# The last 1024 hidden columns of a squared-ReLU MLP by seven products instead of eight

## The chip, the cores and the metric

The kernel runs on one core of a Trainium2 chip. The metric is the device time of one execution in microseconds. A core has TensorE for matmuls, VectorE (DVE), ScalarE (ACT) and GpSimd (POOL) for the rest, and queues from which DMAs are issued: that of SyncE (SP), of GpSimd and of ScalarE. TensorE reads its operands from SBUF and writes to PSUM, which ScalarE and VectorE read.

## The reference, cut to what matters

The reference is one layer of a decoder block on 512 tokens of width 1024: a token mixer (gated linear attention and latent attention in parallel, merged by gates), a layer norm, the MLP, a layer norm. The change lies in the MLP, with `w_ff1` of 1024 x 4096 and `w_ff2` of 4096 x 1024:

```python
h = layer_norm(DEEPNORM_ALPHA * h + mix, ln1_g[l], ln1_b[l])
ff = jnp.square(jax.nn.relu(h @ w_ff1[l])) @ w_ff2[l]
h = layer_norm(DEEPNORM_ALPHA * h + ff, ln2_g[l], ln2_b[l])
```

## The kernel before

Everything is float32. Each operand of a large product is split into a high part `hi` (fp32r, written by ScalarE's copy, L185 in `pump`, L111 in `split`) and a low part `lo` (the rest, by a subtraction on VectorE, L186 or L112). A product is three matmuls: hi x hi, hi x lo, lo x hi, accumulated in PSUM.

**The stream of weights.** All weights are listed ahead in `stream`, in the order in which they are used, as items of 512 KB (128 partitions x 1024 columns). `pump(i)`, called ahead of item `i`, issues the DMAs of items up to `i + DMA_AHEAD` on SP's queue (L173) into one of three `wraw` tiles, and the splits of items up to one further into one of two `whi` and two `wlo` tiles. Items marked `res`, and those whose `home` is `"a"`, go to tiles of the shared pool `"A"` (24 tiles of 4 KB per partition). An item with a `src` has no DMA: its tile is loaded elsewhere. Pool `"B"` has 22 tiles of 2 KB; the split activations `h1T` occupy 16 of them from the layer norm to the end of the first MLP product. PSUM has eight banks, four tagged `mm` and four `px`.

**The order.** Small generators (`spawn`, `tick`) are advanced between matmuls, so that their instructions are listed among them. The list order is a priority. The framework's scheduler then fixes the order of instructions on each engine with its own estimates of time, and an instruction may be issued well ahead of its place in the list if its operands and a buffer are free.

**The MLP.** It goes in four chunks of 1024 hidden columns (`for ci in range(FC)`). In each, the first product (`gemm_fm`, L238 to L240) makes the hidden values with columns on partitions: eight blocks of k, eight blocks of 128 columns, three matmuls of 512 tokens. `ev_h` applies relu (L1296) and a square. In the first three chunks the second product runs by seven products instead of eight (`win_f2`, L1268 to L1270): 14 steps of 12 matmuls, whose weight tiles `wq` are loaded by `win_load` on GpSimd's queue (L1213) and summed by `win_sums`. Its results are copied from PSUM to `ev` tiles (L1280) and added to the rows `res` by accumulating DMAs, again on GpSimd's queue (L1282). In the last chunk `ev_h` squares on ScalarE (L1310) and on GpSimd (L1311) and subtracts on VectorE (L1312), and the second product is plain (`gemm_tm`, L271 to L273, by pairs of token blocks, then the third and the fourth block), ending in the layer norm `ln2`.

**The gate product.** One other product already runs by seven products: the second half of the gates (`gemm_unit` with the key `"g1"`, L1016 to L1018). Its operands `h` and `w` are cut into 2 x 2 quarters. `op_sums` forms the four sums of the quarters of `h` and splits them (L965 to L972); `u_load` loads weight quarters and adds a second one by an accumulating DMA (L988, L990); `u_sum` makes the other weight sums on VectorE (L324). The products follow `FMO`: 11, 21, t1, 22, t2, t3, t4, each of 48 matmuls of 256 tokens. Between them the banks are combined by copies on ScalarE and subtractions on VectorE (L1023 to L1036).

Of the kernel before, what the change touches and what calls it, by code (L numbers as in the profile page):

```python
# [19 lines left out]
P = 128  # L20
T = 512
# [31 lines left out]
def tile_hybrid_block(ctx: ExitStack, tc: tile.TileContext, I, out, dbg=None):  # L53
# [108 lines left out]
    def pump(i):  # L162
        while st["dma"] < min(len(stream), i + 1 + DMA_AHEAD):
            e = stream[st["dma"]]
            st["dma"] += 1
            if "src" in e:
                continue
            raw = A([P, e["nk"], T * 2 // e["nk"]], F32, "wraw")
            for sl, src, cw in e["dmas"]:
                dst = raw[:, sl, :e["n"]]  # L170
                if cw is not None:
                    dst = dst.rearrange("p (h c) -> p h c", c=cw)
                nc.sync.dma_start(dst, src)  # L173
            e["raw"] = raw
        while st["spl"] < min(len(stream), i + 2 + SPLIT_AHEAD):
            e = stream[st["spl"]]
            if st["spl"] > i + e.get("ahead", SPLIT_AHEAD) and not e["res"]:
                break
            nk, n = e["nk"], e["n"]
            hi, lo = [A([P, nk, T * 2 // nk], F32R, w) for w in HOME["a" if e["res"] else e.get("home", "w")]]  # L180
            raw = e["src"]() if "src" in e else e.pop("raw")
            with ExitStack() as gates:
                for g in st["gates"]:
                    gates.enter_context(tc.issue_after(g.ins))
                st["ins"] = act(hi[:, :nk, :n], raw[:, :nk, :n], AF.Copy)  # L185
                vtt(lo[:, :nk, :n], raw[:, :nk, :n], f(hi[:, :nk, :n]), op=ALU.subtract)  # L186
# [121 lines left out]
    UNITS = {"g1": ("w_in", C_G + D)}  # L308
# [8 lines left out]
    def u_src(key, i, j, hf):  # L317
# [4 lines left out]
    def u_sum(key, a, to, hf, x):  # L322
        t = WQ[key, (to, hf)] = WQ[key, (a, hf)]
        vtt(t, t, x, op=ALU.add)  # L324


    for key in UNITS:
        PL[key] = []
        for op, _ in FMO:
            for hf in range(2):  # L330
                PL[key].append(len(stream))
                e = {"nk": 2, "n": T, "res": False}
                if op[0] != "t":
                    e["dmas"] = [(slice(0, 2), u_src(key, int(op[0]) - 1, int(op[1]) - 1, hf), None)]
                else:
                    e["src"] = lambda q=(key, (op, hf)): WQ[q]
                if op == "22":
                    e["post"] = lambda raw, q=(key, "t1", "t2", hf): u_sum(*q, raw)
                elif op == "t2":
                    e["post"] = lambda raw, q=(key, "t2", "t4", hf): u_sum(*q, WQ[key, ("21", q[3])])  # L340
                stream.append(e)
    plan_qr(0)
# [27 lines left out]
    F1 = [((0, 4), (4, 2), (6, 2))] + [tuple((b, 2) for b in range(0, 8, 2))] * 2 + [((0, 4), (4, 4))]  # L370
# [3 lines left out]
    for ci in range(FC):  # L374
# [610 lines left out]
    def u_load(key, op):  # L985
        for hf in range(2):
# [5 lines left out]
    def gemm_unit(key, ops, evac, after=None):  # L992

        bank, e1, e5, u2 = {}, {}, {}, {}
        nk = 2
        for n, (op, ph) in enumerate(FMO):
            items = PL[key][2 * n:2 * n + 2]
            for g in range(2):
                bk = ("a" if ph in (0, 3, 6, 4) else "b", g)
                opens = ph in (0, 2, 1)  # L1000
                if opens:
                    bank[bk] = (PX if ph == 1 else MM)()
                o = bank[bk]
                for hf, it in enumerate(items):
                    pump(it)
                    hi, lo = stream[it]["w"]
                    for pp in range(nk):
                        while len(ops) <= nk * hf + pp:
                            tick(3)
                        xh, xl = ops[nk * hf + pp][ph]  # L1010
                        for a in range(2):
                            c = slice((2 * g + a) * P, (2 * g + a + 1) * P)
                            oa = o[:, a * 256:(a + 1) * 256]
                            first = opens and hf == 0 and pp == 0 and a == 0
                            last = hf == 4 // nk - 1 and pp == nk - 1
                            mm(oa, hi[:, pp, c], xh, start=first, stop=False, skip_group_check=True)  # L1016
                            mm(oa, hi[:, pp, c], xl, start=False, stop=False, skip_group_check=True)  # L1017
                            mm(oa, lo[:, pp, c], xh, start=False, stop=last, skip_group_check=True)  # L1018
                        if pp % 2:
                            tick(3)  # L1020
# [3 lines left out]
                elif ph == 1:  # L1024
                    vtt(e1[g], o, e1[g], op=ALU.add)
                    evac(0, 0, g, e1[g], None)
# [3 lines left out]
                elif ph == 3:  # L1030
# [3 lines left out]
                    evac(1, 0, g, u2[g], None)  # L1034
                elif ph == 6:
                    vtt(e5[g], e5[g], o, op=ALU.subtract)  # L1036
                    evac(1, 1, g, e5[g], None)
                elif ph == 4:
                    evac(0, 1, g, o, None)
            if after:  # L1040
                after(op)

# [209 lines left out]
    def win_f2(ci, hid):  # L1252
        bank = {}
        for n, (op, hf, ph) in enumerate(WIN):
# [28 lines left out]
            if n == 9 and ci + 1 < FC - 1:  # L1283
                win_load(ci + 1)

    WT = {}
    for ci in range(FC):
# [6 lines left out]
        def ev_h(a, ps):  # L1294
            r = B([P, T], F32, "relu")
            act(r, ps, AF.Relu)  # L1296
            if win:
                if a % 2 == 0:
                    hid.append({"R": A([P, 2, T], F32, "hr")})
                ops = hid[-1]  # L1300
                R = ops["R"]
                act(R[:, a % 2, :], r, AF.Square)
                if a % 2:
                    h1 = A([P, 2, 2, 256], F32R, "h1p")
                    split(R[:, :, :256], h1[:, 0], h1[:, 1])
                    ops[0], ops[1] = [(h1[:, 0, i], h1[:, 1, i]) for i in range(2)]
                    spawn(win_hid(R, ops))
                return
# [4 lines left out]
            hid.append(hh)  # L1313
# [15 lines left out]
        else:  # L1329
            bg, bb = bcast_row("ln2_g"), bcast_row("ln2_b")  # L1330
            gemm_tm(PL["f2last"], hid, T, ev_res, tts=(0, 1))
# [67 lines left out]
```

## Time and profile before

| what | value |
|---|---|
| median of three runs | 901.83 us (900.83 to 902.12) |
| profiled execution, its own time | 901.97 us |
| its span | 900.2 us |
| granted TensorE clock | 0.998 |
| instructions on TensorE | 4652 matmuls |
| busy share of VectorE, ScalarE, GpSimd | 65%, 47%, 20% |
| second product of the third chunk | 766.9 to 805.0 us of the span |
| first product of the last chunk | 805.0 to 848.5 us |
| plain second product of the last chunk | from 848.5 us |

The span runs from the first to the last instruction of the profiled execution; the execution's time is 1.8 us longer. Times within the profile are counted from the span's start. In the view of groups, a row gives the line, the engine, the operation and the tiles (out<-in), the count, busy time and mean duration. In the view of waits a row says which engine and line waited for which, in total, how often, and the longest. A row of the timeline gives the start, the duration, the engine and the instruction, and in brackets the idle time before it with what ended it. A row of the table by stretches gives the stretch and its length, then the busy time and count of TensorE, its weight loads, VectorE, ScalarE and GpSimd, then the granted clock, the DMA share and the rate in GB/s.

### The profile page before, as it was taken

Reading aid. Unit: us, or ns where it says so; the run is one execution under the profiler, and the core shown is the slowest. Engines: PE = TensorE matmul, PEld = TensorE weight load, DVE = VectorE, ACT = ScalarE, POOL = GpSimd, SP = SyncE. Lnnn points to the kernel's source line nnn. Section 1 sums busy time; section 2 is a strip of 40 time slices with the busy share of each in tenths; the row PEclk is TensorE's granted clock in tenths of the full one; section 3 lists DMA queues with packets and bytes.
Section 4 is the critical chain, followed back from the end, with each engine's and each line's share of the span. In section 5 each row is a group of like instructions: output and inputs, shape, how many; then the busy total and the mean of one; then the engine's idle time right before and its main releaser. Section 6 shows DMA issues by size and latency. Waiting matters only on the chain.

```text
span 900.2 us, 12161 instructions
## 1 busy us (share of the span) xinstructions
PE 880.9 (98%) x4652; PEld 755.8 (84%) x4652; DVE 585.5 (65%) x953; ACT 427.3 (47%) x729; POOL 178.0 (20%) x196
## 2 busy tenths in 40 slices
PE   5999999999999999999999999999999999999996
PEld 5988888888889988888888888988888888888885
DVE  7835855577876645747756797997557646723565
ACT  5556443443546543445644423466367546733410
POOL 0103442444531010100000002104400520142200
PEclk9999999999999999999999999999999999999999
DMA  7414323216225623121207518005941990594311
GB/s 241 124 47 159 129 65 94 71 47 155 81 71 195 175 88 105 43 60 53 94 24 277 191 49 302 1 1 151 296 115 32 261 243 24 117 209 108 128 68 73
DMA packets 64776, 107.25 MB, mean 119 GB/s; under 512 B 7840, under 2 KB 27680, under 8 KB 64720
## 3 DMA queue, kind: packets, MB, share of 16 engines
q1 hardware_dynamic: 51344, 75.57, 26.3%
q0 software_dynamic: 11456, 27.27, 13.0%
q10 hardware_dynamic: 1920, 3.66, 1.2%
q8 instruction: 36, 0.59, 0.3%
q14 instruction: 20, 0.16, 0.1%
HBM read 89.18 MB, written 4.72 MB: 104 GB/s over the span
## 4 chain that ended last, share of the span: by engine, by line
PE 96%; DVE 2%; DMA 1%; ACT 1%; issue 0%; SPq 0%; DVEq 0%
PE mm L238 14%; PE mm L240 14%; PE mm L239 14%; PE mm L271 7%; PE mm L273 7%; PE mm L272 7%; PE px L1269 2%; PE px L1270 2%; PE px L1268 2%; PE px L723 2%; PE mm L1269 2%; PE mm L1270 2%; PE mm L1268 2%; PE mm L1018 1%; PE mm L1016 1%; PE mm L1017 1%
## 5 line engine op out<-in xcount | busy, mean ns | idle before, releaser
L186 DVE TENSOR_TENSOR wlo<-wraw,whi 128x1024 fp32r<-128x1024 f32 (+1 forms) x102 | 115.3, 1131 | 131.6 <-ACT whi L185 124.0
L185 ACT ACTIVATE whi<-wraw 128x1024 fp32r<-128x1024 f32 (+1 forms) x102 | 98.2, 962 | 109.5 <-PE mm L239 63.3
L238 PE MATMUL mm<-h,whi 128*128 128x512 f32 x352 | 137.6, 392 | 0.0
L239 PE MATMUL mm<-h,whi 128*128 128x512 f32 x352 | 137.3, 390 | 0.0
L240 PE MATMUL mm<-h,wlo 128*128 128x512 f32 x352 | 130.5, 390 | 0.0
L1282 POOL DMA_DIRECT2D res<-ev x48 | 42.1, 1018 | 187.5 <-ACT ev L1280 151.6
L238 PEld LDWEIGHTS mm<-h,whi 128*128 128x128 f32 x352 | 66.0, 188 | 13.5
L240 PEld LDWEIGHTS mm<-h,wlo 128*128 128x128 f32 x352 | 66.0, 188 | 13.5
L239 PEld LDWEIGHTS mm<-h,whi 128*128 128x128 f32 x352 | 66.1, 188 | 13.3
L272 PE MATMUL mm<-wlo,h 128*128 128x512 f32 x128 | 50.3, 393 | 0.0
L273 PE MATMUL mm<-whi,h 128*128 128x512 f32 x128 | 50.1, 392 | 0.0
L271 PE MATMUL mm<-whi,h 128*128 128x512 f32 x128 | 49.7, 403 | 0.0
L185 ACT ACTIVATE xh<-wraw 128x1024 fp32r<-128x1024 f32 (+1 forms) x28 | 27.1, 985 | 36.8 <-PE mm L273 16.5
L662 POOL TENSOR_TENSOR rp<-rp 128x256 f32<-128x256 f32 x32 | 31.6, 987 | 61.2 <-ACT E L667 44.8
L1296 ACT ACTIVATE relu<-mm 128x512 f32<-128x512 f32 x32 | 18.8, 595 | 49.3 <-PE mm L240 49.2
L186 DVE TENSOR_TENSOR wlo<-wq,whi 128x1024 fp32r<-128x1024 f32 x20 | 24.5, 1225 | 24.2 <-ACT whi L185 24.2
L391 POOL TENSOR_TENSOR mv<-mv,mhalf 128x1 f32<-128x1 f32 x4 | 4.6, 1154 | 172.4 <-DVE mv L390 172.4
L186 DVE TENSOR_TENSOR xl<-wraw,xh 128x1024 fp32r<-128x1024 f32 (+1 forms) x28 | 31.2, 1128 | 8.9 <-ACT xh L185 8.7
L669 DVE TENSOR_TENSOR M<-E,qk 128x512 f32<-128x512 f32 x32 | 27.8, 868 | 14.1 <-ACT E L667 14.1
L667 ACT ACTIVATE E<-rp 128x512 f32<-128x512 f32 x32 | 20.4, 638 | 24.9 <-POOL rp L663 24.9
L663 POOL TENSOR_TENSOR rp<-rp 128x256 f32<-128x256 f32 x32 | 28.2, 883 | 8.9 <-ACT q L692 6.7
L273 PEld LDWEIGHTS mm<-whi,h 128*128 128x128 f32 x128 | 24.0, 188 | 5.0
(405 smaller groups left out, 2415.3 us busy)
## 6 DMA issues: line engine op xcount, KB each, us to landing
wraw<-in_w_ff_dram SPq DMA_DIRECT2D x40, 512.0 KB, 4.5
wraw<-in_w_in_dram SPq DMA_DIRECT2D x38, 512.0 KB, 3.5
wq<-in_w_ff_dram POOLq DMA_DIRECT2D x24, 512.0 KB, 9.4
res<-ev POOLq DMA_DIRECT2D x48, 256.0 KB, 6.6
wraw<-in_w_o_gla_dram SPq DMA_DIRECT2D x8, 512.0 KB, 3.8
wraw<-in_w_o_mla_dram SPq DMA_DIRECT2D x8, 512.0 KB, 3.5
wraw<-in_w_out_dram SPq DMA_DIRECT2D x8, 512.0 KB, 3.9
wq<-in_w_in_dram SPq DMA_DIRECT2D x6, 512.0 KB, 5.5
```

The source lines that it names most:

```text
L185: st["ins"] = act(hi[:, :nk, :n], raw[:, :nk, :n], AF.Copy)
L186: vtt(lo[:, :nk, :n], raw[:, :nk, :n], f(hi[:, :nk, :n]), op=ALU.subtract)
L238: mm(o, hi[:, c], xh, start=first, stop=False)
L239: mm(o, hi[:, c], xl, start=False, stop=False)
L240: mm(o, lo[:, c], xh, start=False, stop=last)
L271: mm(o, xh, hi[:, :n], start=opens, stop=False, skip_group_check=share)
L272: mm(o, xh, lo[:, :n], start=False, stop=False, skip_group_check=share)
L273: mm(o, xl, hi[:, :n], start=False, stop=last, skip_group_check=share)
L1268: mm(o, xh[:, c], hi[:, pp], start=opens, stop=False, skip_group_check=True)
L1269: mm(o, xh[:, c], lo[:, pp], start=False, stop=False, skip_group_check=True)
L1270: mm(o, xl[:, c], hi[:, pp], start=False, stop=hf == 1 and pp == 1, skip_group_check=True)
L1282: nc.gpsimd.dma_start(res[tt + t][:, j * T:(j + 1) * T], e, accum_op=ALU.add)
```

## The change

The first product of the last chunk runs by the seven products that the gate product uses: `gemm_unit("f1", hops, ev_u, after1)` in place of two calls of `gemm_fm`. For that:
- Items of a seven-product weight are laid out anew, for the gate product too: four blocks of k by 256 columns (rows of 1 KB) instead of two by 512 (rows of 2 KB), one item for each half `g` of the columns, so that an item is used by one half alone.
- `h1_sums` forms the sums of `h1T` into eight tiles of pool `"A"`. It is spawned after step 10 of the third chunk's second product (`U0`).
- The tiles t1 (after step 8, `U1`), t3 and 21 (after the first product) are loaded by GpSimd's queue, both the load and the accumulation; the gate product keeps SP's queue for the load.
- `fetch` is cut out of `pump`, and called after step 9 (`U2`) for the first two raw tiles.
- The hidden values come in eight pieces of 256 columns by 256 tokens; `ev_u` spreads their relu, square and subtraction over several steps. The multiplication moves from GpSimd to VectorE. `Halves` presents the pieces to the plain second product.

The diff, cut to its core:

```diff
-    def pump(i):
-        while st["dma"] < min(len(stream), i + 1 + DMA_AHEAD):
+    def fetch(n):
+        while st["dma"] < min(len(stream), n):
...
+    def pump(i):
+        fetch(i + 1 + DMA_AHEAD)
...
-    UNITS = {"g1": ("w_in", C_G + D)}
+    UNITS = {"g1": ("w_in", C_G + D), "f1": ("w_ff1", 3 * D)}
...
-        return src[:, 4 * hf + i:4 * hf + i + 3:2, c0 + j * T:c0 + (j + 1) * T]
+        c0 += j * T + g * 256
+        return src[:, i:8:2, c0:c0 + 256]
...
-    F1 = [((0, 4), (4, 2), (6, 2))] + [tuple((b, 2) for b in range(0, 8, 2))] * 2 + [((0, 4), (4, 4))]
+    F1 = [((0, 4), (4, 2), (6, 2))] + [tuple((b, 2) for b in range(0, 8, 2))] * 2 + [()]
...
+            plan_unit("f1")
             plan_zip("f2last", [("w_ff2", 0, fb, True), ("w_ff2", T, fb, True)])
...
-    def u_load(key, op):
-        for hf in range(2):
-            t = WQ[key, (op, hf)] = A([P, 2, T], F32, "wq")
-            nc.sync.dma_start(t, u_src(key, *{"21": (1, 0)}.get(op, (0, 1)), hf))
+    def u_load(key, op, dma=nc.sync.dma_start):
+        for g in range(2):
+            t = WQ[key, (op, g)] = A([P, 4, 256], F32, "wq")
+            dma(t, u_src(key, *{"21": (1, 0)}.get(op, (0, 1)), g))
             if op != "21":
-                nc.gpsimd.dma_start(t, u_src(key, *{"t1": (0, 0), "t3": (1, 1)}[op], hf), accum_op=ALU.add)
+                nc.gpsimd.dma_start(t, u_src(key, *{"t1": (0, 0), "t3": (1, 1)}[op], g), accum_op=ALU.add)
...
+            for g in range(2):
+                bk = ("a" if ph in (0, 3, 6, 4) else "b", g)
                 if opens:
-                    bank[bk] = (PX if ph == 1 else MM)()
+                    bank[bk] = (PX if ph == 1 else (pb or MM) if ph == 2 else MM)()
+                o, it = bank[bk], PL[key, op, g]
+                pump(it)
+                hi, lo = stream[it]["w"]
+                for k in range(4):
+                    while len(ops) <= k:
+                        tick(3)
+                    xh, xl = ops[k][ph]
...
+            if ci == FC - 2 and n == U0:
+                t_h1.append(spawn(h1_sums()))
+            if ci == FC - 2 and n == U2:
+                fetch(PL["f1", "11", 1] + 1)
+            if ci == FC - 2 and n == U1:
+                u_load("f1", "t1", nc.gpsimd.dma_start)
...
+    def h1_new():
+        t = [A([P, 2, 2, 256], F32R, "sh1") for _ in range(2)]
+        return [(x[:, 0], x[:, 1]) for x in t]
+
+    def h1_sums():
+        yield from op_sums(h1T, h1_new, hops)
...
+    U0, U1, U2 = 10, 8, 9
...
-            hh = A([P, 2, T], F32R, "hid0")
-            act(hh[:, 0, :], r, AF.Square)
-            gtt(r, r, r, op=ALU.mult)
-            vtt(hh[:, 1, :], r, f(hh[:, 0, :]), op=ALU.subtract)
...
+            def ev_u(j, i, g, ps, sb):
+                def later():
+                    for _ in range(1 + 4 * i):
+                        yield
+                    r = ps if sb else B([P, T], F32, "relu")
+                    act(r, ps, AF.Relu)
+                    hh = A([P, 2, 2, 256], F32R, "hid0")
+                    act(hh[:, 0], r.rearrange("p (a c) -> p a c", a=2), AF.Square)
+                    yield
+                    vtt(r, r, r, op=ALU.mult)
+                    vtt(hh[:, 1], r.rearrange("p (a c) -> p a c", a=2), f(hh[:, 0]), op=ALU.subtract)
+                    hts[j, i, g] = hh
+                spawn(later())
+
+            def after1(op):
+                if op == "11":
+                    u_load("f1", "t3", nc.gpsimd.dma_start)
+                    u_load("f1", "21", nc.gpsimd.dma_start)
+            gemm_unit("f1", hops, ev_u, after1)
```

More of the change, by code (lines that the diff above doesn't have):

```diff
@@ L1001, in gemm_unit @@
                 if opens:
-                    bank[bk] = (PX if ph == 1 else MM)()
[L1003 to L1020, printed above, removed]
+                    bank[bk] = (PX if ph == 1 else (pb or MM) if ph == 2 else MM)()
@@ L1296, in ev_h @@
             act(r, ps, AF.Relu)
[L1297 to L1308, printed above, removed]
-            hh = A([P, 2, T], F32R, "hid0")
-            act(hh[:, 0, :], r, AF.Square)
-            gtt(r, r, r, op=ALU.mult)
-            vtt(hh[:, 1, :], r, f(hh[:, 0, :]), op=ALU.subtract)
-            hid.append(hh)
+            if a % 2 == 0:
+                hid.append({"R": A([P, 2, T], F32, "hr")})
+            ops = hid[-1]
+            R = ops["R"]
+            act(R[:, a % 2, :], r, AF.Square)
+            if a % 2:
+                h1 = A([P, 2, 2, 256], F32R, "h1p")
+                split(R[:, :, :256], h1[:, 0], h1[:, 1])
+                ops[0], ops[1] = [(h1[:, 0, i], h1[:, 1, i]) for i in range(2)]
+                spawn(win_hid(R, ops))
         for b, w in F1[ci]:
@@ L1330, in tile_hybrid_block @@
             bg, bb = bcast_row("ln2_g"), bcast_row("ln2_b")
+            hts = {}
+            def ev_u(j, i, g, ps, sb):
[16 more added lines that the diff above has]
+            gemm_unit("f1", hops, ev_u, after1)
+            hid = [Halves(hts, j, g, a) for j in range(2) for g in range(2) for a in range(2)]
             gemm_tm(PL["f2last"], hid, T, ev_res, tts=(0, 1))
```

65 lines of the change are left out of this document (43 added, 22 removed).

## The prediction

> **What bounds the kernel now.** I read the page first, its busy shares and its chain of work that ended last.
>
> ```profile
> PE 880.9 (98%) x4652; PEld 755.8 (84%) x4652; DVE 585.5 (65%) x953; ACT 427.3 (47%) x729; POOL 178.0 (20%) x196
> ...
> PE 96%; DVE 2%; DMA 1%; ACT 1%; issue 0%; SPq 0%; DVEq 0%
> ```
>
> TensorE is the bound, and 96% of the chain is matmuls. The view of waits, for TensorE alone, says how much of that could be waiting:
>
> ```profile
> PE px L406 <- ACT x L395: 9.5, 1, 9.5
> ...
> PE mm L1018 <- DVE wlo L186: 0.5, 1, 0.5
> ```
>
> After the start, no wait is over 0.5 us. So the time falls only if the matmuls take less, and any new wait of TensorE adds itself in full. The matmuls are read from the timeline of TensorE by their starts, since the printed durations (0.39, 0.28) overlap. First the product that is replaced, its start and its end, then the gate product that already runs by seven products:
>
> ```profile
> 805.02 0.39 PE L238 MATMUL mm<-h,whi 128*128 128x512 f32 x1
> ...
> 848.32 0.39 PE L240 MATMUL mm<-h,wlo 128*128 128x512 f32 x1
> 848.54 0.39 PE L271 MATMUL mm<-xh,hid 128*128 128x512 f32 x1
> ```
>
> ```profile
> 288.14 0.28 PE L1016 MATMUL mm<-sh,whi 128*128 128x256 f32 x1
> 288.26 0.28 PE L1017 MATMUL mm<-sh,whi 128*128 128x256 f32 x1
> ...
> 312.29 0.38 PE L1018 MATMUL mm<-h,wlo 128*128 128x256 f32 x1 [0.48 <-DVE wlo L186]
> ...
> 317.90 0.40 PE L271 MATMUL mm<-whi,latT 128*128 128x256 f32 x2
> ```
>
> The replaced product has 8 blocks of k, 8 of columns and 3 terms, 192 matmuls of 512 columns, in 848.54 - 805.02 = 43.52 us: 226.7 ns each, without a gap. A matmul of 256 columns starts 0.12 us after the one before, more than half of 226.7.
>
> **TensorE's part.** Seven products over 4 blocks of k, 4 of columns and 3 terms are 336 matmuls of 256 columns. At 0.120 us they take 40.3 us, so 3.2 us go. By the Trainium skill (TensorE: Matmul & The Clock Gate, "Back-to-back issue gap") a lone matmul of N columns takes N/2.4 + 2.5 ns, 215.8 and 109.2 ns here, and the saving would be 41.4 - 36.7 = 4.7 us; the trace does not agree, with 226.7 and 120 ns at a granted clock of 0.998.
>
> Gaps come off this. From 288.14 to 317.90 the gate product issues its last five products, 240 matmuls, in 29.76 us where 28.8 are due: 0.96 lost, 0.64 of it ahead of the row at 312.29. The cause is the pace of the splits, seen in the timeline of ACT and DVE:
>
> ```profile
> 297.22 1.06 ACT L185 ACTIVATE whi<-wq 128x1024 fp32r<-128x1024 f32 x1 [1.68 <-PE mm L1017]
> 298.31 1.23 DVE L186 TENSOR_TENSOR wlo<-wq,whi 128x1024 fp32r<-128x1024 f32 x1 [2.00 <-ACT whi L185]
> 299.86 1.06 ACT L185 ACTIVATE whi<-wq 128x1024 fp32r<-128x1024 f32 x1 [1.58 <-PE mm L1017]
> ```
>
> One weight item feeds 24 matmuls, 2.88 us. With two buffers for each half, the next split can only begin when the item before is done, and it takes 299.54 - 297.22 = 2.32 us. Slack is 0.56 us: a vector operation of 1.22 us that starts just ahead of `wlo` costs up to 0.66. Fourteen items replace eight, and what shares the two engines grows:
> - ScalarE: 14 x 1.06 for splits, 6 copies x 0.59, 8 relu x 0.60 and 8 squares x 0.63, 28.2 of 40.3 us.
> - VectorE: 14 x 1.23, 4 weight sums x 1.22, 6 combinations x 0.69, 8 multiplications that leave GpSimd and 8 subtractions at 0.69 (L965 and L1312 without contention): 37.2 us. The first split lies before the product, and the last quarter pair (2 x 1.38) after it, so 33 of 40.3, 82%. The gate product had 17.2 of 25 us between 285 and 310, 69%.
>
> Bounds for the lost time: none (it fits), or each of the four sums and eight multiplications hits a `wlo`, 4 x 0.66 + 8 x 0.13 = 3.7 us. The nearest row is the gate product; I take its 0.96 as 1.0.
>
> The gate product itself changes too: each of its items now carries four blocks of k for half the columns, so it is used once and freed. Its matmuls, splits and bytes stay. It could win back its 0.96 or lose as much through DMA rows of 1 KB; I take zero, since its items already came free after about 24 matmuls (297.22 to 299.86).
>
> **The sums of h.** For each of four pairs `op_sums` adds two 512-column sums, four of 256 and two splits: 8 x 0.70 + 16 x 0.41 + 8 x 0.68 = 17.6 us on VectorE, 8 x 0.62 = 5.0 on ScalarE. They are spawned after step 10 of the preceding second product; steps take 2.72 us from 766.94, so at 796.9, and their tiles come free earlier. The first two products need no sum, so the third, at 805.0 + 4 x 2.88 = 816.5, is their due time. The stages show the room:
>
> ```profile
> 790.00:803.00 13.00, 13.00 (x59) 10.74 (x59) 2.45 (x2) 5.87 (x9) 5.50 (x7) 1.00 0.99 203
> 803.00:814.00 11.00, 11.00 (x50) 9.13 (x49) 2.45 (x2) 2.82 (x4) 3.51 (x4) 1.00 0.92 181
> ```
>
> The third number after TensorE's two is VectorE: 2.45 us busy in 13, 2.45 in 11. From 790 to 816.5 about 21 us are idle. Two more splits, two combinations and a weight sum take 5 of them; 16 remain for 17.6 us, and the last block of k is due only 2.2 us later. Cost zero, but nothing is spare: if the sums begin only at 796.9, 5 us of those 16 are gone, and TensorE waits up to 5 us. I keep 0 to 5.
>
> **The weight tiles.** GpSimd's queue loads t1 at step 8 (two tiles of 512 KB, two accumulating DMAs), then t3 and 21 after the first product. These move past the `res<-ev` DMAs (L1282) of the same queue. The fetch of raw tiles costs nothing and brings nothing: three `wraw` DMAs were issued from 775.3 to 786.5, before step 9 at 791.4. The two `bcast_row` DMAs already go out at 773.1 and 777.7. The hidden values of tokens 256 to 511, ready last, are first read 96 x 0.2267 = 21.8 us into the closing product, which covers their relu and squares.
>
> ```profile
> DMA to landing us min/median/max: 6.4/10.6/13.2
> ```
>
> This is the landing time of the eight `wq` loads in the second chunk (700 to 712), next to the same `res<-ev` traffic. Those began 16.6 us after their product's start (701.6); the same offset here is 783.5. Load and accumulation in a row take about 21 us, 804.7; the slowest, 26, 810. The split of t1 is due at about 814. So it is hidden, with 4 us spare. By the Trainium skill (DMA: Bandwidth & Descriptors, "Anatomy of one DMA — SWDGE (gpsimd) path") a DMA takes 2.0 us + bytes/436e3, 3.2 us each, and the sum would lie there after 6.4 us; the rows do not agree.
>
> **Sum.** The profiled execution took 901.97 us, 900.2 of span and 1.8 around it. Minus 3.2, plus 1.0, is 2.2 off: 899.8. The median of the runs is 901.83, 0.14 below, so 899.6. A change of 0.2% is 1.8 us, about what a measurement of this kernel can tell: faster ends at 900.0, slower begins at 903.6.
>
> **Rivals.**
> - *The matmuls shrink and the splits give it back.* VectorE at 82%, half a microsecond of slack per item, and a schedule fixed ahead in which one late operation delays all behind it speak for it; that the gate product lost only 0.96 speaks against. With the 3.7 us of the upper bound, and some of the 0 to 5 of late h sums, lost time lies between 1.4 and 5.0 us, and the run between 900.0 and 903.6; in the middle, 901.8.
> - *The accumulating DMA holds GpSimd's queue* (slower). The accumulation must wait for its load, 10.6 us by the row above, and stands in one queue with `res<-ev`. Behind it the `ev` tiles stay occupied, ScalarE waits in order at its next `ev` copy with the weight splits behind that, and TensorE follows. Against it: in the first chunk, eight loads among the same DMAs raised the landing of `res<-ev` to 10.2 us (622 to 660) and TensorE did not wait; but none of those loads was waited for by the next DMA of the queue. Room: the last `ev` copy of the fourth product ended at 794.1, its bank is needed at 799.6, 5.5 us. If the queue is held for both tiles' loads, 13.2 us, TensorE stalls 7.7, and 7.7 - 2.2 = 5.5 slower: 907.3. It decides the sign beyond 5.5 + 2.2 = 7.7 us of holding, and passes the 0.2% at 9.5.
> - *Nothing is shortened* would need a 256-column matmul of over 43.52/336 = 129.5 ns; 240 rows at 124.0 including gaps exclude it, and I give it no chance of its own.
>
> **How the numbers follow.** Forecast, shorter matmuls with few gaps: 0.57. Splits give it back: 0.23. Queue held: 0.20. These are the three chances. The range begins at 898.0, nearly all of 3.2 us and part of the gate product's 0.96 won (897.7 in full), and reaches over the second case to 904.0, which leaves out most of the third and a little below. For the forecast alone it is 898.0 to 900.0.
>
> **What would show it.** Right: TensorE x4796 on the page; 256-column matmuls at 0.12 us from about 805; the last product of the second MLP starting 2.2 us earlier than 848.54; waits `PE <- DVE wlo` of about 1 us in the new stage; t1 tiles landed before 814. Wrong: waits of TensorE between 785 and 805 with ScalarE at `ev` (queue held); waits on `sh1` or `wq` at the third product, 816.5 (late sums); many waits at `wlo` (splits); a granted clock below 0.998.

## The result, and the profile after

The changed kernel takes 902.64 us in the median of 17 runs (901.37 to 905.86), the kernel before 901.44 in 17 runs beside it (900.79 to 903.44). The ratio is 1.0018, with a 95% interval of 1.0009 to 1.0026. It lies within the 0.2% that the prediction called no change, near its upper edge, on the other side of 1 than forecast, and the time lies inside the stated 898.0 to 904.0 us. The profiled execution took 904.8 us, of which 902.9 is the span: one of the longer ones, 2.2 above the median. Line numbers are shifted in the new kernel: the seven products are L1019 to L1021, the `ev` copies L1289, the evictions L1291, the weight loads L994 and L996, the weight sums L328.

The page first, busy shares and chain:

```profile
PE 880.7 (98%) x4796; PEld 761.3 (84%) x4796; DVE 616.7 (68%) x1009; ACT 440.0 (49%) x749; POOL 177.8 (20%) x198
...
PE 91%; DMA 5%; DVE 2%; issue 1%; ACT 1%; POOL 1%; SPq 0%; DVEq 0%; POOLq 0%; ACTq 0%
```

There are 144 more matmuls and no more busy time, and matmuls no longer make 96% of the chain: DMAs have 5%. The view of waits for TensorE from 785 to 850 us, then:

```profile
PE mm L1021 <- DVE wlo L189: 3.2, 2, 2.6
PE mm L1277 <- ACT ev L1289: 0.4, 1, 0.4
PE px L1021 <- DVE wlo L189: 0.3, 1, 0.3
```

A single wait for `wlo` took 2.6 us; before, none after the start was over 0.5. The timeline of TensorE shows it, and what follows:

```profile
824.16 0.39 PE L1021 MATMUL mm<-sh,wlo 128*128 128x256 f32 x1 [2.56 <-DVE wlo L189]
824.38 0.28 PE L1019 MATMUL mm<-sh,whi 128*128 128x256 f32 x1
824.50 0.28 PE L1020 MATMUL mm<-sh,whi 128*128 128x256 f32 x1
...
825.18 0.41 PE L1019 MATMUL mm<-sh,whi 128*128 128x256 f32 x1
825.39 0.41 PE L1020 MATMUL mm<-sh,whi 128*128 128x256 f32 x1
...
828.38 0.29 PE L1019 MATMUL mm<-sh,whi 128*128 128x256 f32 x1
828.50 0.28 PE L1020 MATMUL mm<-sh,whi 128*128 128x256 f32 x1
```

The starts lie 0.12 us apart, then 0.21 from 825.18 to 828.38, then 0.12 again: 15 matmuls lose 0.09 each, 1.4 us more. The stages say why; after TensorE's two pairs come DVE, ACT and POOL, then the granted clock, the busy share of the DMA engines (1 is all sixteen; the view's sums reach a little over 1) and GB/s. First the kernel before, then the changed one:

```profile
795.00:805.00 10.00, 10.00 (x45) 8.28 (x45) 3.68 (x3) 4.81 (x8) 3.75 (x5) 1.00 0.94 187
805.00:815.00 10.00, 10.00 (x46) 8.26 (x44) 1.23 (x1) 1.80 (x3) 3.51 (x4) 1.00 0.88 186
815.00:825.00 10.00, 10.00 (x46) 8.29 (x45) 2.45 (x2) 2.18 (x3) 0.00 (x0) 1.00 0.30 86
825.00:835.00 10.00, 10.00 (x46) 8.29 (x45) 6.15 (x5) 6.11 (x11) 5.10 (x4) 1.00 0.29 98
```

```profile
795.00:805.00 10.00, 10.00 (x45) 8.26 (x44) 9.26 (x17) 7.52 (x14) 7.71 (x8) 1.00 1.10 189
805.00:815.00 10.00, 9.26 (x74) 8.81 (x74) 7.85 (x13) 6.54 (x11) 6.33 (x9) 1.00 1.12 235
815.00:825.00 10.00, 7.17 (x58) 6.77 (x57) 7.46 (x9) 5.96 (x8) 1.83 (x3) 1.00 1.08 276
825.00:835.00 10.00, 10.00 (x74) 10.00 (x73) 6.34 (x7) 3.38 (x4) 1.98 (x2) 0.83 1.10 289
```

The clock fell to half after the long wait (0.50 from 825.0 to 828.3). The DMA engines, at 0.94, 0.88, 0.30 and 0.29 before, are full from 795 to 835. VectorE, 12% to 37% busy in the first three stages before, is now at 75% to 93%. The timeline of VectorE around the long wait:

```profile
817.49 0.69 DVE L1371 TENSOR_TENSOR e<-e 128x512 f32<-128x512 f32 x1 [0.18 <-ACT hid L1369]
820.54 1.23 DVE L328 TENSOR_TENSOR wq<-wq,wraw 128x1024 f32<-128x1024 f32 x1 [2.36 <-DMA wraw<-in_w_ff_dram]
...
822.88 1.22 DVE L189 TENSOR_TENSOR wlo<-wq,whi 128x1024 fp32r<-128x1024 f32 x1
```

`wlo` of t1's second half was due, but VectorE's fixed order has the sum of t1 and raw tile 22 ahead of it, and that tile had not landed. From issue to landing the raw tiles (`wraw`, issues from 798 to 830) took, in the kernel before and in the changed one:

```profile
DMA to landing us min/median/max: 3.5/3.7/3.9
```

```profile
DMA to landing us min/median/max: 9.2/11.6/16.9
```

With the starts of TensorE's matmuls, the account of this execution is: all gaps over 0.08 us after 760 sum to 6.9 us (0.7 at 794.7, 1.8 in three places from 809 to 816, 2.8 at 824, the slow clock's 1.4, 0.2 at 840). The shorter matmuls take 3.2 off. The product ahead of the unit began 0.7 earlier (766.2 instead of 766.9). Together, -0.7 - 3.2 + 6.9 = 3.0; the last matmul starts 3.1 later, at 895.39 instead of 892.26.

### The profile page after: what moved, and what is told of

The parts are those of the page before. It is cut to its first block, busy times and chain, and to the rows that moved or that the text cites. A ratio compares the mean times of both kernels' runs of the same rounds, so it can differ in the third digit from the quotient of the medians.

```text
span 902.9 us, 12545 instructions
## 1 busy us (share of the span) xinstructions
PE 880.7 (98%) x4796; PEld 761.3 (84%) x4796; DVE 616.7 (68%) x1009; ACT 440.0 (49%) x749; POOL 177.8 (20%) x198
## 4 chain that ended last, share of the span: by engine, by line
PE 91%; DMA 5%; DVE 2%; issue 1%; ACT 1%; POOL 1%; SPq 0%; DVEq 0%; POOLq 0%; ACTq 0%
PE mm L241 12%; PE mm L243 12%; PE mm L242 12%; PE mm L274 7%; PE mm L276 7%; PE mm L275 7%; DMA res<-ev 4%; PE mm L1021 2%; PE mm L1020 2%; PE mm L1019 2%; PE px L1278 2%; PE px L1277 2%; PE px L1279 2%; PE px L729 2%; PE mm L1278 1%; PE mm L1277 1%
## 5 line engine op out<-in xcount | busy, mean ns | idle before, releaser
L189 DVE TENSOR_TENSOR wlo<-wraw,whi 128x1024 fp32r<-128x1024 f32 (+1 forms) x100 | 112.7, 1128 | 110.5 <-ACT whi L188 102.8
L241 PE MATMUL mm<-h,whi 128*128 128x512 f32 x288 | 112.7, 392 | 0.0
L242 PE MATMUL mm<-h,whi 128*128 128x512 f32 x288 | 112.4, 390 | 0.0
L243 PE MATMUL mm<-h,wlo 128*128 128x512 f32 x288 | 107.1, 390 | 0.0
L1291 POOL DMA_DIRECT2D res<-ev x48 | 43.7, 1090 | 188.3 <-ACT ev L1289 152.3
L243 PEld LDWEIGHTS mm<-h,wlo 128*128 128x128 f32 x288 | 54.0, 188 | 11.1
L241 PEld LDWEIGHTS mm<-h,whi 128*128 128x128 f32 x288 | 54.0, 188 | 11.0
L242 PEld LDWEIGHTS mm<-h,whi 128*128 128x128 f32 x288 | 54.1, 188 | 10.7
L189 DVE TENSOR_TENSOR wlo<-wq,whi 128x1024 fp32r<-128x1024 f32 x28 | 34.2, 1223 | 21.9 <-ACT whi L188 21.9
L668 POOL TENSOR_TENSOR rp<-rp 128x256 f32<-128x256 f32 x32 | 31.6, 989 | 61.1 <-ACT E L673 44.8
L1021 PE MATMUL mm<-sh,wlo 128*128 128x256 f32 x128 | 37.2, 290 | 2.6 <-DVE wlo L189 2.6
L188 ACT ACTIVATE whi<-wq 128x1024 fp32r<-128x1024 f32 x28 | 29.6, 1056 | 17.9 <-PE mm L1020 10.4
L675 DVE TENSOR_TENSOR M<-E,qk 128x512 f32<-128x512 f32 x32 | 27.8, 868 | 14.1 <-ACT E L673 14.1
L1020 PE MATMUL mm<-sh,whi 128*128 128x256 f32 x128 | 36.9, 288 | 0.0
L1019 PE MATMUL mm<-sh,whi 128*128 128x256 f32 x128 | 36.9, 288 | 0.0
```

What stands on the lines that cost most here:

```text
L241: mm(o, hi[:, c], xh, start=first, stop=False)
L242: mm(o, hi[:, c], xl, start=False, stop=False)
L243: mm(o, lo[:, c], xh, start=False, stop=last)
L1019: mm(oa, hi[:, k, c], xh, start=opens and k == 0 and a == 0, stop=False, skip_group_check=True)
L1020: mm(oa, hi[:, k, c], xl, start=False, stop=False, skip_group_check=True)
L1021: mm(oa, lo[:, k, c], xh, start=False, stop=k == 3, skip_group_check=True)
```

## The experiments

Two theories to begin with. *Late raw tile*: the added loads overfill the DMA engines, and what needs a tile waits. *VectorE is full*: the sums of h and the multiplications leave it no room. Every ratio below is against the kernel before on the same chip. Times within a profile count from its own span's start, so they can be shifted between runs: the product ahead of the unit begins between 764.9 and 766.9.

**The gate product's layout alone.**

```diff
 # kernel before, with items of four blocks of k x 256 columns for the gate product only
-    UNITS = {"g1": ("w_in", C_G + D), "f1": ("w_ff1", 3 * D)}
+    UNITS = {"g1": ("w_in", C_G + D)}
...
```

> The kernel before with one part of the change: the items of the gate product carry four blocks of k by 256 columns instead of two by 512; the last chunk's first product stays as it was. In the changed kernel's profile the gate product lost 0.37 us between matmuls where it lost 1.10 before, and ended 0.78 us sooner counted from its own start. If that belongs to the layout, time is 0.7 us less than before, ratio 0.999 to 0.9995. If it was chance of one execution, ratio 1.000.

901.13 us (900.66 to 901.57), ratio 0.9995 (0.9987 to 1.0004). That is 0.4 us less, not told from none; the loss is in the new unit and what feeds it.

**Order on VectorE, and less to load.** The first puts the weight sum behind the split; the second loads 21 once, for its product and for the last sum; the third leaves out the loads of t3 and of the second 21, and sets the tiles to zero instead.

```diff
 # k1_behind
-        vtt(t, t, x, op=ALU.add)
+        with tc.issue_after(st["lo"].ins):   # the last wlo subtraction
+            vtt(t, t, x, op=ALU.add)
 # k2_once
...
+                u_load("f1", "21")               # with t1, on SP's queue; item 21 reads this tile
...
-                    u_load("f1", "21", nc.gpsimd.dma_start)
 # k3_noload
-                    u_load("f1", "t3", nc.gpsimd.dma_start)
-                    u_load("f1", "21", nc.gpsimd.dma_start)
+                    for g in range(2):
+                        WQ["f1", ("t3", g)] = t = A([P, 4, 256], F32, "wq")
+                        nc.gpsimd.memset(t, 0.0)
+                        WQ["f1", ("21", g)] = t
```

> The changed kernel, with each weight sum of VectorE queued behind the split of the item it belongs to (a no-wait edge on VectorE), so that the sum with raw tile 22 no longer stands ahead of the low part of t1's second half. Theory 'late raw tile': the DMA queues are overfull from 785 to 837 us, raw tile 22 lands 11.6 us after its issue, VectorE waits for it with the due split behind, TensorE waits 2.7 us and then runs 3.2 us at half clock (1.5 us). Then most of these 4.2 us go in the profile; the split of 22 itself still waits for the same tile, so 0.5 to 1.5 us stay. Time 899.5 to 901, ratio to the kernel before 0.997 to 0.9995. Rival 'VectorE is full' (sums of h and the multiplications moved from GpSimd): the order of one sum changes nothing in the total, ratio 1.001 to 1.003, the wait reappears at another split.

903.83 us (901.86 to 906.28), ratio 1.0025 (1.0014 to 1.0035). The 2.6 us wait is gone, and others stand in its place: 1.7 at 814.4 and 1.2 at 836.8. The order around the late tile is not the cause.

> The changed kernel, with quarter 21 of the weights loaded once: SP's queue loads it into the two shared-pool tiles that the later weight sum reads, the split of product 21 reads the same tiles, and the second load on GpSimd's queue is gone (1 MB less). Raw tiles 22 then use the third raw buffer and the first one freed, and are issued two items sooner. Theory 'late raw tile': raw tile 22 lands before it is needed, the 2.7 us wait and the half clock go, time 898.5 to 900.5, ratio 0.9965 to 0.999. Rival 'VectorE is full': 1.001 to 1.003, since VectorE's work is the same.

901.71 us (900.13 to 903.82), ratio 1.0003 (0.9994 to 1.0011): 1.4 us less than the change. The largest gaps left in its profile are 1.3 and 1.0 us, for `wlo` at 808.8 and 812.8; 0.8 at 799.0 and 0.6 at 822.1 stand beside them.

> The changed kernel without the loads of t3 and of the second 21: the two tiles are set to zero on GpSimd instead, 3 MB of DMA less, so products t3 and t4 use wrong weights. The order on VectorE is the same as in the changed kernel, instruction by instruction, with the sum of raw tile 22 still ahead of the split. Theory 'late raw tile': raw tile 22 lands in 5 to 8 us instead of 11.6, the wait at that split shrinks from 2.7 to under 1 us and the clock stays full, time 898.5 to 901, ratio 0.9965 to 0.9995. If the landing is late because of the traffic before it (the accumulations of the residual, t1) and not of these loads, the wait stays and the ratio is above 1.0. Rival 'VectorE is full': no change, 1.001 to 1.003.

900.70 us (899.61 to 903.12), ratio 0.9997 (0.9988 to 1.0006): 1.9 less. So loads cost time, but without 3 of their 5 MB the 3 us are still not there.

**Sums sooner, and no loads at all.** `U0` is the step of the preceding product at which the sums of h are spawned.

```diff
 # e6_sums6 (U0 only), e9_once6 (21 loaded once as well)
-    U0, U1, U2 = 10, 8, 9
+    U0, U1, U2 = 6, 8, 9
 # e7_quiet, and e8_quiet6 with U0 = 6: also t1 by memset, like t3 and 21 above
-                u_load("f1", "t1", nc.gpsimd.dma_start)
+                for g in range(2):
+                    WQ["f1", ("t1", g)] = t = A([P, 4, 256], F32, "wq")
+                    nc.gpsimd.memset(t, 0.0)
```

> The changed kernel with none of the unit's extra loads: t1, t3 and the second copy of 21 are set to zero by GpSimd (left out: 6 MB of transfers, half of them accumulating; the output is that of a product without these sums). 'Traffic': the raw tiles of 21 and 22 land in under 6 us again, the waits for whi and wlo at 814 and 824 are gone, and the time falls by 2.5 to 4 us from the changed kernel, to 898 to 900; with the last loads alone left out it fell by about 1.9. The spread between executions falls from 4 us to under 1.5 us. 'VectorE is full': nothing that VectorE does has changed, so the time stays above 901.5.

900.85 us (900.40 to 901.63), ratio 0.9990 (0.9981 to 0.9999). The edit leaves out 5 MB, 2 of them accumulating (its expectation says 6 and half). The loads' share of the loss is the difference to 1.0018, 2.5 us. The executions here lie within 1.2 us, those of the change within 4.5. But 2 us are still missing, and VectorE's timeline at the first wait (1.3 us, until 808.75) shows the sums of h ahead of the due `wlo`:

```profile
804.45 1.29 DVE L971 TENSOR_TENSOR hraw<-h,h 128x512 f32<-128x512 f32 x2
805.65 1.29 DVE L112 TENSOR_TENSOR sh<-hx,sh 128x512 fp32r<-128x512 f32 x2
...
807.53 1.22 DVE L189 TENSOR_TENSOR wlo<-wraw,whi 128x1024 fp32r<-128x1024 f32 x1
```

> The changed kernel with the sums of h started at step 6 of the third chunk's second product instead of step 10, some 13 us sooner; nothing else is touched. In the profiled executions so far, PE waited for a wlo at 808.8 and 812.8 (0.77 + 0.29 us in the changed kernel, 1.31 + 0.95 with 21 loaded once) while VectorE was still at the sums of h. 'Order on VectorE': these waits go, 1 to 2 us less than the changed kernel, about 901. 'Late raw tile' (traffic): the waits at 814 to 825 for tiles 21 and 22 stay or grow by as much as the first ones shrink, so within 0.5 us of the changed kernel, about 902.3. If the sums compete with the hidden sums of the second product instead, new waits appear between 781 and 797 and the time is over 903.

908.23 us (906.06 to 908.91), ratio 1.0066 (1.0054 to 1.0079). The third case of its expectation, new waits, and more than priced. The adds began 2.8 us sooner (786.8 instead of 789.6), the first split of a sum only 1.0 (794.7 instead of 795.7), and `xl` of the preceding product was late twice (0.8 and 0.9 us). Starting sooner is no cure: something else holds the splits. ScalarE stood 7.4 us at an `ev` copy, until 793.5.

> The one before this with the sums of h started at step 6 as well (the same loads left out). Both causes are taken away here, so what is left is the saving of the matmuls themselves: 3.2 us by the sum of the prediction and about 0.4 from the gate product's layout, so 897.8 to 899 if nothing else stalls. If it stays above 900.5, the saving of the matmuls is not there, or a third stall (the evictions at the end of the second product, the closing product) takes it. 'VectorE is full' expects this one to be faster than the kernel without loads by more than 1.5 us, 'traffic' by less than 1 us.

902.33 us (900.78 to 903.34), ratio 1.0007 (0.9998 to 1.0016). A miss for both theories, 1.5 us slower than with `U0` at 10; the profiled execution, 900.78, was the shortest of all, so its profile doesn't show where. Its executions lie 2.6 us apart, without any of the loads.

> A kernel with the whole computation: 21 loaded once (sooner, by SyncE's queue, and used both for its product and for the last sum) and the sums of h from step 6. Against 21 loaded once alone (901.7 where the kernel before took 901.4), 'order on VectorE' expects the waits of 1.31 and 0.95 us at 808.8 and 812.8 to go and the time to be 899.5 to 900; 'traffic' alone expects 901 to 902, with waits for raw 22 in their place.

902.15 us (900.94 to 904.58), ratio 1.0004 (0.9996 to 1.0013): no gain over 21 loaded once alone.

**The bare unit, and the loads without the sums.**

```diff
 # e13_bare (on e7_quiet) and e12_nosums (on the change)
-        yield from op_sums(h1T, h1_new, hops)
+        for p in range(4):
+            blk = {(i, h): tuple(part(h1T[2 * p + i], w, slice(256 * h, 256 * h + 256)) for w in range(2))
+                   for i in range(2) for h in range(2)}
+            hops.append({0: blk[0, 0], 1: blk[1, 0], 4: blk[1, 1], 2: blk[0, 1], 3: blk[0, 1], 5: blk[0, 0], 6: blk[1, 0]})
+            yield
```

> The changed kernel without its extra loads (t1, t3 and the second copy of 21 set to zero by GpSimd) and without the sums of h (the products that use one take a plain block of h): both left out, so the output differs. What is left is the unit's matmuls, splits and evictions. 'The saving is real, two side costs eat it': no wait of PE above 0.3 us from 785 to 850 and 3.5 us under the kernel before (3.1 from the matmuls, 0.4 from the gate product's layout), a ratio of 0.9955 to 0.9970. 'The saving is not there' (256-column matmuls lose it among themselves): above 0.9985, as in the kernel with the loads alone left out (0.9990).

898.68 us (898.36 to 899.45), ratio 0.9968 (0.9956 to 0.9981). The saving is real: 2.9 us, the gate product's layout included. In the view of waits for TensorE, 785 to 850, one line is left, though none over 0.3 us was expected:

```profile
PE mm L1021 <- DVE wlo L189: 0.5, 1, 0.5
```

From here to the kernel without loads the sums of h cost 0.0022, 2.0 us (the two intervals just touch, at 0.9981).

> The changed kernel with all its loads, but without the sums of h (the products that use one take a plain block of h; the sums are left out). If the sums and the loads cost independently, this is the bare unit plus what the loads cost (2.5 us by the difference of the changed kernel and the one without loads): a ratio of 0.9985 to 1.0000. If the loads only hurt because VectorE is late already, it is within 0.001 of the bare unit. If VectorE's sums are innocent it stays at 1.0018 as the changed kernel.

909.32 us (908.50 to 910.24), ratio 1.0085 (1.0071 to 1.0099). Far outside every case. The edit did more than it says: the sums' tiles no longer occupy the pool, so the loads of t3 and 21 went out 26 us sooner than in the changed kernel (812.43), by the timeline of GpSimd:

```profile
786.84 3.43 POOL L994 DMA_DIRECT2D wq<-in_w_ff_dram  x4
```

They fell among the evictions, and TensorE waited for raw tiles and splits from 807 to 830 (gaps of 9.8 us in all). It says nothing on the sums, but it shows what these loads cost there.

**What holds the sums.** ScalarE's timeline in the kernel before, at its longest stand for an eviction in this product, then in the changed kernel:

```profile
793.51 0.60 ACT L1280 ACTIVATE ev<-px 128x512 f32<-128x512 f32 x1 [2.65 <-DMA res<-ev]
```

```profile
787.40 1.06 ACT L188 ACTIVATE xh<-wq 128x1024 fp32r<-128x1024 f32 x1
794.03 0.60 ACT L1289 ACTIVATE ev<-mm 128x512 f32<-128x512 f32 x1 [5.57 <-DMA res<-ev]
...
795.00 1.15 ACT L111 ACTIVATE sh<-hx 128x512 fp32r<-128x512 f32 x2
```

ScalarE stands 5.6 us at an `ev` copy, until an accumulating eviction has landed and given its tile back (median landing 8.5 us from 766 to 815, 5.0 before), and the high parts of the sums, L111, are behind it in order. VectorE then does most of the sums after 795. Left out in the next two runs: the evictions of the products 21, T1 and T2 of the preceding second product, 6 of 16 DMAs.

```diff
 # e18_quietfree (on e7_quiet) and e17_free (on the change)
+                        if ci < FC - 2 or ph not in (1, 2, 3):
                             nc.gpsimd.dma_start(res[tt + t][:, j * T:(j + 1) * T], e, accum_op=ALU.add)
```

> The changed kernel without its extra loads (ratio 0.9990), and in the third chunk's second product without the accumulating evictions of the products 21, T1 and T2 (6 of 16 DMAs left out, their copies by ScalarE kept; the sums of h are all there). 'ScalarE held by the evictions': the wait of 4 us for DMA res<-ev before the copy at 793 goes, the first sh split moves from 795.6 to about 791, the sums end 3 us or more sooner, the waits of TensorE at 808.8 and 812.1 go, and the ratio comes down to the bare unit's, 0.9965 to 0.9975. 'VectorE has no room': the waits at 808 to 812 stay over 1 us and the ratio is above 0.9982.

897.86 us (897.24 to 898.42), ratio 0.9961 (0.9947 to 0.9974): the bare unit's time, with all the sums. The stages 785 to 805 and the one wait that is left to TensorE:

```profile
785.00:795.00 10.00, 10.00 (x46) 8.29 (x45) 9.51 (x16) 6.41 (x10) 1.13 (x2) 1.00 0.34 105
795.00:805.00 10.00, 10.00 (x53) 8.60 (x53) 9.93 (x20) 6.14 (x10) 3.41 (x5) 1.00 0.81 153
```

```profile
PE mm L1021 <- DVE wlo L189: 0.5, 1, 0.5
```

VectorE is 95% and 99% busy, where it is 75% and 93% in the changed kernel: the sums just fit if they may start. The first split of a sum stands at 791.0 on ScalarE, the last sum ends at 809.5 on VectorE, 3.2 us sooner than in e7_quiet (1.9 counted from the start of the product ahead of the unit). Raw tiles are not the reason: they landed in 5.4 us in the median, against 5.7. So "VectorE is full" is excluded as the first cause of the sums' 2 us; the order on ScalarE, where the splits stand behind copies that wait for evictions, is shown. Why an eviction takes so long is not shown. Full DMA engines are not needed for it: in e7_quiet they were at 0.65 and 0.78 from 785 to 790 and 790 to 795 and ScalarE stood 4.1 us, in the kernel before at 0.79 and 1.09, and it stood 2.65.

> The changed kernel with all its loads and sums, without the same six evictions (left out). 'Full DMA engines': 1.5 MB of accumulating transfers less between 784 and 796, so the raw tiles of 21 and 22 land in under 8 us, the wait of 5.6 us at ev goes, and the ratio falls from 1.0018 to 0.9985 or below. If only the loads after 812 (t3 and the second 21) matter for the raw tiles, it stays above 1.0000.

900.25 us (899.42 to 902.61), ratio 0.9992 (0.9983 to 1.0001): 2.3 us less than the change, short of what was expected. The 5.6 us at `ev` and the waits at 809 to 816 are gone. But raw tiles still took up to 14.1 us to land (7.4 in the median). The loads of t3 and 21 went out at 806.5 here; VectorE waited 2.7 us for a raw tile at 822.6, the due `wlo` stood behind that, and TensorE waited 1.6 us at 826.3. So the loads cost their 2.8 us (against 0.9961) by a second way, the one of the long wait at 824 in the change.

**Loads moved to where the DMA engines idle.** Before, their share was 0.00 from 750 to 765 and 0.09 from 765 to 775.

```diff
 # e10_once4: 21 loaded once, t1 and 21 loaded at step 4; e11_once48: and U0 = 8
-    U0, U1, U2 = 10, 8, 9
+    U0, U1, U2 = 10, 4, 9
```

> The whole computation, 21 loaded once, and t1 and 21 loaded at step 4 of the third chunk's second product instead of step 8, before most of the accumulating evictions that fill the DMA engines from 784 on. 'Traffic': raw tiles 21 and 22 land sooner, 1 us less than with 21 loaded once alone (ratio 1.0003), 0.999. 'GpSimd's queue' (the accumulation of t1 waits for its load in front of the evictions): PE waits for ev at 780 to 795 and the ratio is 1.001 or more.

900.48 us (899.63 to 902.13), ratio 0.9989 (0.9980 to 0.9998): as expected in time, and under both kernels. Not by the way expected: the remaining raw tiles still took 9.9 us in the median. In the profiles, the sums of h began at 787.9 instead of 793.4 with 21 loaded once, and the waits of TensorE after 760 came to 2.4 us instead of 3.6. Why the sums began sooner stays open. ScalarE stood at an `ev` copy here too, 5.0 us until 798.04, and the next split of a sum stands behind it, at 800.25.

> As the one before this, with the sums of h from step 8 of the second product instead of step 10 (5.4 us sooner). If the sums can be fitted in between the second product's own sums and the unit's splits, the wait of 1.3 us at 808.8 goes and the ratio is 0.9975 to 0.9985. If VectorE has no such place from 785 to 812, a wait for xl at 797 to 804 takes its stead, as with step 6 (0.84 and 0.9 us), and the ratio is 0.9995 or more.

901.80 us (900.17 to 903.04), ratio 1.0001 (0.9992 to 1.0009). No gain from sooner sums while the evictions run, as with step 6; the gap is 1.3 us at 805.3, for `wlo`, and not for `xl`.

**Is the rest order or load on VectorE?** In e10_once4, a wait of 1.4 us for `wlo` at 811.6 is the largest left. Two versions let products 11 and 21 start without the sums and spawn these later.

```diff
 # e14_due11 (U0 = 11) and e15_due12 (U0 = 12), on e10_once4; hops holds the plain blocks from the start
-                    while len(ops) <= k:
+                    while len(ops) <= k or ph not in ops[k]:
                         tick(3)
...
```

> The version with t1 and 21 loaded at step 4 (ratio 0.9989), but products 11 and 21, which use plain blocks of h, no longer wait for the sums, and these start at step 12, so that 21's splits stand ahead of the last group of them on VectorE. 'Order': the wait of 1.4 us for wlo at 811.6 falls below 0.5 us, and the ratio is 0.997 to 0.998. 'VectorE is full': the work is only moved on, product t1 waits for sh1 or for its own wlo from 816 to 824 by 1 us or more, and the ratio is 0.9985 or above.

902.89 us (901.41 to 904.90), ratio 1.0017 (1.0008 to 1.0025). The wait at 811.6 is gone, and gaps stand behind it instead: 1.4 us at 819.0 for `sh`, 0.8 at 819.9 for `wlo`, 0.7 at 825.3. The granted clock was at 0.50 for 3.4 us from 821.3. The work is moved on, as "VectorE is full" has it. But the evictions were all there, and e18_quietfree shows that the same sums fit without six of them; whether the load of VectorE or the wait at `ev` is behind the gaps here, no run tells.

> The same with the sums from step 11, between the two. On VectorE only half a group of the sums is left behind 21's splits. 'Order': a ratio between 0.9975 and 0.9989. 'VectorE is full': 0.9985 or above.

900.62 us (899.26 to 903.47), ratio 0.9987 (0.9979 to 0.9996). The same as e10_once4, and the wait is still there (1.4 us at 811.5). These two are the best versions of the whole computation, some 1.1 us under the kernel before and 2.6 under the change; the intervals don't tell them apart.

**The multiplication on GpSimd again.**

```diff
 # e16_gpmul, on e10_once4
-                    vtt(r, r, r, op=ALU.mult)
+                    gtt(r, r, r, op=ALU.mult)
```

> The version with t1 and 21 loaded at step 4, with the squares of the unit's hidden values for the low parts (eight multiplications, 0.6 us of VectorE each) taken by GpSimd. They start after 812, behind the wait at 811.6, so 'order' expects no change of that wait and a ratio within 0.0007 of 0.9989. 'VectorE is full in the unit' expects the 0.57 us at 820.9 to go and 0.5 to 1 us less.

909.93 us (907.94 to 910.34), ratio 1.0085 (1.0072 to 1.0098). A miss, and the clearest wait of the study. GpSimd's timeline, then VectorE's, then TensorE's:

```profile
822.60 2.66 POOL L996 DMA_DIRECT2D wq<-in_w_ff_dram  x2 [9.60 <-DMA wq<-in_w_ff_dram]
824.76 2.56 POOL L1372 TENSOR_TENSOR e<-e 128x512 f32<-128x512 f32 x2
```

```profile
826.36 1.51 DVE L1373 TENSOR_TENSOR hid<-e,hid 128x512 fp32r<-128x512 f32 x1 [7.16 <-POOL e L1372]
```

```profile
830.20 0.58 PE L1021 MATMUL mm<-sh,wlo 128*128 128x256 f32 x1 [7.35 <-DVE wlo L189]
```

GpSimd waits 9.6 us to issue t3's accumulation until its load has landed. The multiplications stand behind it, VectorE waits 7.2 us for the first of them, the splits stand behind VectorE, and TensorE waits 7.4. The change's move of the multiplications to VectorE is what avoids this. Whether they cost anything there stays open.

## Why the prediction was wrong

**TensorE's part** held. 336 matmuls at 0.12 us: the bare unit, 2.9 us (1.7 to 4.0) under the kernel before, agrees with 3.2, less its gaps, plus what the layout may have won. **The lost gaps**, taken as 1.0, were 0.6 in the unit both in the bare unit's profile and in e18_quietfree; the bare unit lost 0.3 more ahead of it, at 793. **The gate product's layout**, taken as zero, measured -0.4, not told from zero.

**The sums of h** failed: "Cost zero, but nothing is spare." They cost about 2.0 us. The room was counted on VectorE alone, and there the count was right: in e18_quietfree they fit, at 95% and 99%. It left out that each sum is split first by ScalarE, whose order holds `ev` copies that wait for evictions. Such a wait could be read before, in the row at 793.51 above: 2.65 us for DMA `res<-ev`, with nothing behind it then that made TensorE wait. The start was wrong too, 789.6 and not 796.9, since VectorE ran ahead of the step that spawned the sums; it was no help.

**The weight tiles** failed, though the step that was checked held: t1's accumulations went out at 796.0 and 797.4, and t1 was not late. The same DMAs were priced by whether they land in time, and nothing was charged for whom they delay. DMA engines were at 0.99 and 0.92 in the two stages that the prediction showed, and 5 MB of loads came in beside them, in place of 1 MB of raw tiles. The raw tiles landed in 11.6 us in the median, where it was 3.7 before and 5.7 in the changed kernel without these loads (e7_quiet). The loads cost 2.5 us. "Costs nothing and brings nothing" looked only at the raw tiles' issue.

So the sum: -2.2 predicted; measured, -2.9 for the bare unit, +2.0 for the sums and +2.5 for the loads, together 1.6. These steps add up to the measured 0.0018 by construction, each being the difference to the run before it; that the loads cost 2.8 where the sums fit (e17_free against e18_quietfree) goes with two separate costs.

**The rivals.** *The splits give it back* came closest in time (its middle was at the time before, the change measured 1.2 above), and the measured time lies within its 900.0 to 903.6. Its picture of a late vector operation ahead of a due `wlo` is what the timelines at 808.75 (e7_quiet) and 824 (the change) show. But the splits' own pace, from which it took its price, was not the cause: with the same splits, multiplications and combinations, e13_bare and e18_quietfree lost under 1 us in the unit. What was late were the sums and a raw tile. *The accumulating DMA holds GpSimd's queue* had the right chain in part, `ev` tiles occupied and ScalarE waiting in order with splits behind, but not the cause: the wait at `ev` was 5.3 us in e13_bare, with no loads. TensorE lost 0.7 us by it directly, at 794.7, not 7.7. Its queue did hold in e16_gpmul, at another place.

**What would show it** served well: 4796 matmuls, 0.12 us, waits at `wlo` instead of `sh`. The clock, named as a sign of error, was at 0.50 after the long wait.

## What to carry to other kernels

When transfers are added where the DMA engines are already busy, price not only whether they land in time but whose transfers they delay, and what stands behind those waits on in-order engines. Room on one engine is worth nothing if another engine must serve each step first: follow the whole chain of the added work (here VectorE, ScalarE, VectorE) through the waits that the old profile shows as costless. To find the cause of a loss, strip the added work to the part that saves, then add one cost at a time; and look at where the freed buffers send the other DMAs.

## What the runs showed of the hardware

- In five of the profiles TensorE's granted clock fell to 0.50 ahead of the last matmul, for 3.4 us (6.8 in e16_gpmul). In four of them it fell around the end of, or within, one long wait: 2.44 us in e6_sums6, 2.56 in the change, 2.82 in e12_nosums, 7.35 in e16_gpmul. In e15_due12 the longest wait near it was 1.2 us, with one of 0.5 right after. It stayed at 1.00 after 1.6 us in e17_free, and after 1.6 and 0.8 us close together in k1_behind and k3_noload. So the length of a wait alone does not tell, and the runs give no threshold. The Trainium skill (TensorE: Matmul & The Clock Gate, "HAM oscillation — how this bites in real kernels") warns of idle gaps over about 3.4 us. The traces here show shorter ones to be enough.
- How long a transfer takes depended on what else ran, at one size: 512 KB raw tiles issued from 798 to 830 landed after 3.7 us in the median in the kernel before, with the DMA engines at 0.63 over this stretch, after 5.7 in e7_quiet, at 0.78, and after 11.6 in the change, at 1.09. The first have rows of 2 KB and the others of 1 KB; what the rows make of it was not tested apart.
- Executions of a kernel with the added loads differ by 2.5 to 4.5 us (11 runs and more each), without them by 1.2 in e7_quiet, 2.6 in e8_quiet6 and 2.7 in the kernel before. So the spread is not the loads' alone.
